# Output projection of the token mixers by pairs of column blocks, three of eight k-tile pairs with seven block products

## The chip, the cores and the metric

The kernel runs on one core of a Trainium2 chip. The metric is device microseconds from the first to the last instruction of that core, the median of several runs; the kernel before took 1666.72 us (three runs, 1664.29 to 1666.83). A profile is one execution, recorded by the hardware profiler; its times are microseconds from the start of its span. TensorE is PE in the rows (PEld its weight loads), VectorE is DVE, ScalarE is ACT, GpSimd is POOL, SyncE is SP.

## The reference, cut to what matters

One decoder layer on 256 tokens of width 2048, in float32. The change touches the lines marked with arrows.

```python
mixed = g_m * (y_m @ w_up_m) + g_r * (y_r @ w_up_r) + g_s * (y_s @ w_up_s)
h = x + mixed @ w_out                                    # <- output projection, 2048 x 2048
hn = rmsnorm(h, norm_ffn_g)
h = h + (silu(hn @ ffn_w_gate) * (hn @ ffn_w_up)) @ ffn_w_down   # <- gate and up: 2048 x 5632 each
h = h + (p @ ple_w_proj) * sigmoid(rmsnorm(h, norm_ple_g) @ ple_w_gate)
out = rmsnorm(h, final_norm_g)
```

## The kernel before

**Precision.** Every float32 operand is split into a high part, rounded to the matmul's type by a cast on ACT, and a low part, the difference, made on DVE. A product is three matmuls of 128x512: high x high, low x high, high x low. `split` (L190) does this for activations, `chunk` (L113) for weights; `mm2` (L139) issues the three matmuls in two parts, the third after the low part of the weights is due.

**Weights.** All weights lie in one array `wall` in the order in which they are used, cut into chunks of 1 MB: four tiles of 128x512. `load` (L102) brings one with a single DMA on SP's queue into a ring of three raw buffers. A chunk is split in two halves of 128x1024, each into a `whi` and a `wlo` buffer of which there are three each, so splitting can run some half chunks ahead of PE and no further. `layout` (L1392) writes the array on the host.

**The output projection (L1178 to L1186).** The mixed activations, transposed and split, are `mT[n]` (`mh`, `ml`). Four column blocks of 512 follow one another. For each, two tiles of x are loaded into `h` by ACT's queue, `gemm_tm` (L156) goes over 16 k-tiles in four chunks and two token tiles, 96 matmuls into two PSUM banks of the pool `mm` (four banks, so the next block has two others), DVE adds the banks onto `h`, and `h_block` (L1157) prepares the next stage: a sum of squares on ACT (`jk`), eight transposes on PE into two banks of the pool `sm` (four banks), and their splits, four `hhi` on ACT and four `hlo` on DVE, each 128x256. After the last block `rstd_of` (L1172) gives the norm's factors, with one operation on POOL.

**The FFN's gate and up (L1212 to L1307).** Eleven blocks, each one block of gate columns beside one of up columns. K is taken in eight pairs `u` of k-tiles, in the order `ORDER = (3, 4, 0, 5, 1, 6, 2, 7)`, one chunk for each. For `u` in `SEVEN = (0, 1, 2)` the 2x2 block product is formed with seven block products instead of eight (Winograd's form): `seven` (L1232) makes sums of the weight tiles, two on POOL (L1240, L1244; `tsum`) and two on DVE, and splits 7 tiles in place of 4; the activations' sums are made once before the first block (L1213 to L1222: `af`, four `sf`, then the split into `sh` and `sl`). Such a chunk takes 21 matmuls, a plain one 24. The plain products and three of the seven go to the four banks of `mm` (M2, M4, M3, M8), the others to the four banks of `sm` (M1, M7, M5, M6). After u=2 the latter are merged by one copy on ACT and four adds on DVE; after the last chunk four more adds on DVE bring in M2, M4, M3, M8. Then the gating (`sg`: two tanh on ACT, four operations on DVE), eight transposes and four copies into `hid`.

**The order of the work.** The Tile framework schedules at build time: each engine gets its instructions in an order chosen from their priority (program order; what stands under `high_priority`, such as loading and splitting weights and the merges, goes first) and from when its operands and buffers are ready. Buffers of one pool and tag are handed out and waited for by semaphores. The pool `b2` (L95, `t2`) holds 16 tiles of 128x512: `h`, `jk`, `af`, `sf`, `m1s`, `u`, `v`, `sg` and others. The pools `mp` and `pb` of the mixing part are closed at L1193 and L1194, and those of the FFN (`hid`, `dn`, `gu`) take their place.

Of the kernel before, what the change touches and what calls it, by code (L numbers as in the profile page):

```python
# [9 lines left out]
F32 = mybir.dt.float32  # L10
# [7 lines left out]
FFN = 5632  # L18
S5Q = 2
NKT = 16  # L20
# [17 lines left out]
ORDER = (3, 4, 0, 5, 1, 6, 2, 7)  # L38
SEVEN = (0, 1, 2)
# [35 lines left out]
def trunk(ctx: ExitStack, tc: tile.TileContext, xT, x, pT, wall, vecs, csts, s5b, s5c, gfin, out, dbg=None):  # L75
# [114 lines left out]
    def split(hi, lo, src, gain=None):  # L190
# [4 lines left out]
        else:  # L195
            nc.scalar.activation(out=hi, in_=src, func=AF.Identity if not isinstance(gain, float) else AF.Copy, scale=gain)
            nc.vector.scalar_tensor_tensor(out=lo, in0=src, scalar=gain, in1=hi.bitcast(F32), op0=ALU.mult, op1=ALU.subtract)

# [979 lines left out]
    for n in range(4):  # L1178
        xb = []
        for t in range(2):  # L1180
            h[t, n] = t2("h")
            nc.scalar.dma_start(out=h[t, n], in_=x[t * 128:(t + 1) * 128, n * 512:(n + 1) * 512])
        ps = gemm_tm(lambda k: mT[k // 4][0][:, k % 4, :], lambda k: mT[k // 4][1][:, k % 4, :], NKT)
        for t in range(2):
            tt(h[t, n], h[t, n], ps[t], ALU.add)
        h_block(n, hT, "gffn", ssq1)  # L1186
# [18 lines left out]

    SF = {}  # L1212
    for u in SEVEN:  # L1213
        af = t2("af").rearrange("p (a t) -> p a t", a=2)
        sf = t2("sf").rearrange("p (a t) -> p a t", a=4)
        tt(af, hh[:, 2 * u:2 * u + 2, :].bitcast(F32), hl[:, 2 * u:2 * u + 2, :].bitcast(F32), ALU.add)
        tt(sf[:, 0], af[:, 0, TS[1]], af[:, 1, TS[1]], ALU.add)
        tt(sf[:, 1], sf[:, 0], af[:, 0, TS[0]], ALU.subtract)
        tt(sf[:, 2], af[:, 0, TS[0]], af[:, 0, TS[1]], ALU.subtract)
        tt(sf[:, 3], af[:, 1, TS[0]], sf[:, 1], ALU.subtract)  # L1220
        SF[u] = tuple(gu.tile([128, 4, 128], F32R, name=q + "%d" % u) for q in ("sh", "sl"))
        split(*SF[u], sf)  # L1222

    def tiled(r):

        n = r.shape[1]
        hi = ring.tile([128, 2, 512], F32R, name="whi", tag="whi", bufs=3)[:, 0:n]
        lo = ring.tile([128, 2, 512], F32R, name="wlo", tag="wlo", bufs=3)[:, 0:n]
        split(hi, lo, r)
        return [(hi[:, q], lo[:, q]) for q in range(n)]  # L1230

    def seven():  # L1232

        if not loaded:
            load()
        raw, _ = loaded.pop(0)
# [11 lines left out]
    def A(u, t, k):  # L1248
        return hh[:, 2 * u + k, TS[t]], hl[:, 2 * u + k, TS[t]]

    for b in range(11):
# [3 lines left out]
        def prods(ops, last):  # L1255

            n_ = {q: max(i for i, o in enumerate(ops) if o[0] == q) for q in {o[0] for o in ops}}
            for part in range(2):
                for i, (q, a, w) in enumerate(ops):
                    mm2(M[q], *a, *w, part, q not in done, last and part == 1 and i == n_[q], True)  # L1260
                    if part == 0:
                        done.add(q)
# [242 lines left out]
```

## Time and profile before

| what | value |
|---|---|
| median of three runs | 1666.72 us (1664.29 to 1666.83) |
| the profiled execution | 1664.86 us |
| its span, first to last instruction | 1663.1 us |
| granted TensorE clock, mean | 0.998 of full speed |
| PE / PEld / DVE / ACT / POOL busy | 1641.0 / 1380.4 / 1276.8 / 908.7 / 184.8 us |
| output projection, its first matmul to the first of the FFN | 742.32 to 835.15 us |
| first FFN block | 835.15 to 878.97 us |

Busy time is the time in which an engine had an instruction at work. Ends of matmuls are modelled, so their spacing, the distance from one start to the next, says more than their duration. A number behind an arrow in a row is the time that an engine sat idle before the instruction, with what released it.

### The profile page before, as it was taken

How to read it: one execution, taken by the hardware profiler on the slowest of the kernel's cores; microseconds unless marked ns; L12 is line 12 of the kernel's file. 1: busy time of each engine (PE TensorE's matmuls, PEld its weight loads, DVE VectorE, ACT ScalarE, POOL GpSimd, SP SyncE). 2: the span in 40 equal slices, each digit the busy share in tenths (PEclk: the TensorE clock that was granted, in tenths of full speed). 3: DMA queues.
4: the chain of work that ended last, by engine and by line, in shares of the span. 5: the costliest groups of instructions: out<-in, count | busy, mean ns of one | idle time of the engine just before them, and what ended most of it. 6: DMA issues, size and time to landing. Idle time of an engine off the chain costs nothing.

```text
span 1663.1 us, 23487 instructions
## 1 busy us (share of the span) xinstructions
PE 1641.0 (99%) x9255; PEld 1380.4 (83%) x9255; DVE 1276.8 (77%) x1590; ACT 908.7 (55%) x1141; POOL 184.8 (11%) x131
## 2 busy tenths in 40 slices
PE   8999999999999999999999999999999999999997
PEld 8999889987888888888877888888888888888886
DVE  6999776969988545575589988888888867666565
ACT  6465566555645434444465555555555656656454
POOL 1100100100000000000032322332233000000000
PEclk9999999999999999999999999999999999999999
DMA  9655544555454444555544555555555655555553
GB/s 363 196 171 175 171 152 183 189 187 190 164 194 159 149 158 152 178 190 194 213 176 181 190 198 203 202 203 192 189 190 190 232 184 197 180 200 185 219 186 118
DMA packets 49455, 313.69 MB, mean 189 GB/s; under 512 B 5824, under 2 KB 9152, under 8 KB 12736
## 3 DMA queue, kind: packets, MB, share of 16 engines
q1 hardware_dynamic: 43488, 304.59, 50.7%
q0 software_dynamic: 3840, 3.15, 1.1%
q10 hardware_dynamic: 2016, 4.46, 0.8%
q8 instruction: 72, 1.18, 0.3%
q14 instruction: 39, 0.32, 0.1%
HBM read 306.93 MB, written 2.10 MB: 186 GB/s over the span
## 4 chain that ended last, share of the span: by engine, by line
PE 94%; DVE 3%; issue 1%; ACT 1%; DMA 1%; POOL 0%; SPq 0%; POOLq 0%; DVEq 0%
PE mm L142 23%; PE mm L143 23%; PE mm L145 23%; PE mm L149 4%; PE mm L152 4%; PE mm L150 4%; PE M L145 2%; PE M L142 2%; PE M L143 2%; DVE wlo L129 1%; DMA raw<-in_wall 1%; PE sm L544 1%; DVE wlo L194 1%; PE sm L1306 0%; PE mm L135 0%
## 5 line engine op out<-in xcount | busy, mean ns | idle before, releaser
L128 ACT CAST whi<-raw 128x1024 fp32r<-128x1024 f32 (+1 forms) x496 | 518.1, 1049 | 552.5 <-PE mm L143 393.4
L129 DVE TENSOR_TENSOR wlo<-raw,whi 128x1024 fp32r<-128x1024 f32 (+1 forms) x496 | 612.2, 1238 | 240.2 <-ACT whi L128 221.4
L143 PE MATMUL mm<-whi,alo 128*128 128x512 f32 x512 | 201.2, 393 | 0.0
L142 PE MATMUL mm<-whi,ahi 128*128 128x512 f32 x512 | 201.0, 393 | 0.0
L142 PE MATMUL mm<-whi,hhi 128*128 128x512 f32 x506 | 198.1, 392 | 0.3 <-DVE m1s L219 0.3
L143 PE MATMUL mm<-whi,hlo 128*128 128x512 f32 x506 | 196.8, 389 | 0.0
L149 PE MATMUL mm<-ahi,whi 128*128 128x256 f32 x576 | 143.3, 286 | 7.8 <-ACT whi L128 7.8
L145 PE MATMUL mm<-wlo,hhi 128*128 128x512 f32 x506 | 146.5, 393 | 0.8 <-DVE wlo L194 0.8
L150 PE MATMUL mm<-alo,whi 128*128 128x256 f32 x576 | 142.7, 285 | 0.0
L145 PE MATMUL mm<-wlo,ahi 128*128 128x512 f32 x512 | 139.2, 392 | 0.0
L142 PE MATMUL mm<-whi,dh 128*128 128x512 f32 x352 | 130.2, 389 | 0.0
L143 PE MATMUL mm<-whi,dl 128*128 128x512 f32 x352 | 130.2, 389 | 0.0
L149 PEld LDWEIGHTS mm<-ahi,whi 128*128 128x128 f32 x576 | 111.4, 194 | 8.8 <-ACT whi L128 8.0
L145 PEld LDWEIGHTS mm<-wlo,hhi 128*128 128x128 f32 x506 | 94.9, 188 | 24.0 <-DVE wlo L194 4.7
L142 PEld LDWEIGHTS mm<-whi,hhi 128*128 128x128 f32 x506 | 95.0, 188 | 23.1 <-issue 3.8
L142 PEld LDWEIGHTS mm<-whi,ahi 128*128 128x128 f32 x512 | 96.1, 188 | 21.2 <-issue 1.2
L143 PEld LDWEIGHTS mm<-whi,alo 128*128 128x128 f32 x512 | 96.1, 188 | 20.9 <-issue 1.2
L145 PEld LDWEIGHTS mm<-wlo,ahi 128*128 128x128 f32 x512 | 95.6, 188 | 20.6 <-issue 0.4
L150 PEld LDWEIGHTS mm<-alo,whi 128*128 128x128 f32 x576 | 111.4, 194 | 0.4 <-issue 0.4
L143 PEld LDWEIGHTS mm<-whi,hlo 128*128 128x128 f32 x506 | 95.0, 188 | 19.6
L1244 POOL TENSOR_TENSOR tsum<-raw,tsum 128x512 f32<-128x512 f32 x33 | 86.8, 2629 | 115.6 <-DVE tsum L219 110.4
L1240 POOL TENSOR_TENSOR tsum<-raw 128x512 f32<-128x512 f32 x33 | 56.0, 1696 | 381.9 <-PE mm L145 177.5
(536 smaller groups left out, 2842.0 us busy)
## 6 DMA issues: line engine op xcount, KB each, us to landing
raw<-in_wall SPq DMA_DIRECT2D x283, 1024.0 KB, 4.8
xrow<-in_x SPq DMA_DIRECT2D x2, 1024.0 KB, 8.7
h<-in_x ACTq DMA_DIRECT2D x8, 256.0 KB, 3.2
xraw<-in_xT SPq DMA_DIRECT2D x3, 512.0 KB, 10.7
ub<-Bh POOLq DMA_DIRECT2D x16, 64.0 KB, 3.8
ub<-uh POOLq DMA_DIRECT2D x16, 64.0 KB, 3.7
gft<-in_gfin ACTq DMA_DIRECT2D x1, 1024.0 KB, 6.0
out_dram<-fin SPq DMA_DIRECT2D x4, 256.0 KB, 3.2
```

The lines of the kernel that those rows point to most:

```text
L128: nc.scalar.copy(out=hi[:, q, :], in_=r)
L129: nc.vector.tensor_tensor(out=lo[:, q, :], in0=r, in1=hi[:, q, :].bitcast(F32), op=ALU.subtract)
L142: nc.tensor.matmul(ps, ah, wh, start=first, stop=False, skip_group_check=skip)
L143: nc.tensor.matmul(ps, al, wh, start=False, stop=False, skip_group_check=skip)
L145: nc.tensor.matmul(ps, ah, wl, start=False, stop=last, skip_group_check=skip)
L149: nc.tensor.matmul(ps, wh, ah, start=first, stop=False, skip_group_check=skip)
L150: nc.tensor.matmul(ps, wh, al, start=False, stop=False, skip_group_check=skip)
L152: nc.tensor.matmul(ps, wl, ah, start=False, stop=last, skip_group_check=skip)
L194: nc.vector.tensor_tensor(out=lo, in0=src, in1=hi.bitcast(F32), op=ALU.subtract)
L544: nc.tensor.matmul(psy[32 * j:32 * j + 32, a * 256:(a + 1) * 256], cc[:, ri, js_, :], G["s5x"][q][ri][:, a, :], start=ri == 0, stop=ri == ...
L1240: nc.gpsimd.tensor_tensor(out=ts_[:, 0], in0=raw[:, 3], in1=raw[:, 0], op=ALU.subtract)
L1244: nc.gpsimd.tensor_tensor(out=ts_[:, 2], in0=raw[:, 1], in1=ts_[:, 1], op=ALU.subtract)
```

## The change

The output projection takes two column blocks at a time, as the FFN takes gate and up: one function `gemm_pair` now serves both. Three of eight k-tile pairs go by seven products. The sums of the mixed activations (`MS`) are made ahead of the first pair; their split parts lie in tiles of the mixing part that are no longer read (`room_pb`). The results are added onto `h` in two steps: the merged M1, M7, M5, M6 after u=2, and M2, M4, M3, M8 at the end. `h_block` runs for both blocks of a pair after the pair. The sums of h for the FFN (`SF`) stand where they stood. The FFN's first block takes its k pairs in the order `ORDER0`, the other ten in `ORDER`; `tsum` of the FFN moves from the pool `gu` to the pool `hid`. On the host the chunks of `w_out` and of the first FFN block are laid out accordingly.

```diff
 ORDER = (3, 4, 0, 5, 1, 6, 2, 7)
+ORDER0 = (3, 0, 1, 2, 4, 5, 6, 7)
 SEVEN = (0, 1, 2)
...
+    def sums(sf, a):
+        tt(sf[:, 0], a[:, 0, TS[1]], a[:, 1, TS[1]], ALU.add)
+        tt(sf[:, 1], sf[:, 0], a[:, 0, TS[0]], ALU.subtract)
+        tt(sf[:, 2], a[:, 0, TS[0]], a[:, 0, TS[1]], ALU.subtract)
+        tt(sf[:, 3], a[:, 1, TS[0]], sf[:, 1], ALU.subtract)
+    def sums_of(hi, lo, room):
+        af = t2("af").rearrange("p (a t) -> p a t", a=2)
+        sf = t2("sf").rearrange("p (a t) -> p a t", a=4)
+        tt(af, hi.bitcast(F32), lo.bitcast(F32), ALU.add)
+        sums(sf, af)
+        split(*room, sf)
+        return room
...
+    def gemm_pair(A, S, order, by7, room, prep=None, onto=None):
...
+                if end:
+                    with tc.high_priority():
+                        m1, u2, u3, u4, v4 = (t2(q) for q in ("m1s", "u2", "u3", "u4", "v4"))
+                        nc.scalar.copy(out=m1, in_=M[1])
+                        tt(u2, M[6], m1, ALU.add)
+                        tt(u3, M[7], u2, ALU.add)
+                        tt(u4, M[5], u2, ALU.add)
+                        tt(v4, M[5], u3, ALU.add)
+                    res = (m1, u3, u4, v4)
+                    if onto is not None:
+                        for o, r in zip(onto, res):
+                            tt(o, o, r, ALU.add)
+                        res = onto
...
+        with tc.high_priority():
+            for o, q in zip(res, (2, 4, 3, 8)):
+                tt(o, M[q], o, ALU.add)
+        return res
...
-    for n in range(4):
-        xb = []
-        for t in range(2):
-            h[t, n] = t2("h")
-            nc.scalar.dma_start(out=h[t, n], in_=x[t * 128:(t + 1) * 128, n * 512:(n + 1) * 512])
-        ps = gemm_tm(lambda k: mT[k // 4][0][:, k % 4, :], lambda k: mT[k // 4][1][:, k % 4, :], NKT)
-        for t in range(2):
-            tt(h[t, n], h[t, n], ps[t], ALU.add)
-        h_block(n, hT, "gffn", ssq1)
+    MS = {u: sums_of(*(q[:, 2 * (u % 2):2 * (u % 2) + 2, :] for q in mT[u // 2]), room_pb(u)) for u in SEVEN}
+    for n in (0, 2):
+        for m in (n, n + 1):
+            for t in range(2):
+                h[t, m] = t2("h")
+                nc.scalar.dma_start(out=h[t, m], in_=x[t * 128:(t + 1) * 128, m * 512:(m + 1) * 512])
+        gemm_pair(lambda u, t, k: tuple(q[:, 2 * (u % 2) + k, TS[t]] for q in mT[u // 2]), sum_of(MS), ORDER, SEVEN, tsum_t8,
+                  onto=(h[0, n], h[1, n], h[0, n + 1], h[1, n + 1]))
+        for m in (n, n + 1):
+            h_block(m, hT, "gffn", ssq1)
...
-    SF = {}
-    for u in SEVEN:
...
+    SF = {u: sums_of(hh[:, 2 * u:2 * u + 2, :], hl[:, 2 * u:2 * u + 2, :], room_of(gu, "sf%d" % u)) for u in SEVEN}
     for b in range(11):
...
+        c11, c21, c12, c22 = gemm_pair(act_of(hh, hl), sum_of(SF), ORDER if b else ORDER0, SEVEN, tsum_of(hid_p))
...
-    blocks(a["w_out"][0])
+    wo = a["w_out"][0]
+    for n in (0, 1024):
+        pair(wo[:, n:n + 512], wo[:, n + 512:n + 1024], ORDER)
```

The parts of `gemm_pair` that are left out are the FFN block's loop as it was (L1252 to L1292), and `tiled` and `seven` have only moved; `seven` now takes its `tsum` tile from the function `room`.

## Rows read from the trace of the kernel before

**Rows 1.** From the page: busy time, share of the span and instruction count of PE and DVE; the granted clock in 40 slices of the span, in tenths; the chain that ended last, by engine.
```profile
PE 1641.0 (99%) x9255; PEld 1380.4 (83%) x9255; DVE 1276.8 (77%) x1590; ACT 908.7 (55%) x1141; POOL 184.8 (11%) x131
PEclk9999999999999999999999999999999999999999
PE 94%; DVE 3%; issue 1%; ACT 1%; DMA 1%; POOL 0%; SPq 0%; POOLq 0%; DVEq 0%
```
**Rows 2.** Busy time by stretches: the output projection, the first 26 us of the FFN, its first and second block, and a settled stretch of one block's length. Columns: stretch and its length, busy us and instructions of PE, PEld, DVE, ACT and POOL, granted clock, DMA share, GB/s.
```profile
742.32:835.15 92.83, 92.83 (x425) 76.25 (x424) 52.31 (x59) 44.78 (x61) 0.00 (x0) 1.00 0.56 199
835.15:861.46 26.31, 25.72 (x116) 20.56 (x115) 26.19 (x43) 16.59 (x24) 11.70 (x6) 1.00 0.44 158
835.15:878.97 43.82, 43.22 (x192) 34.74 (x191) 41.62 (x60) 27.09 (x36) 15.12 (x7) 1.00 0.50 180
878.97:922.00 43.03, 42.30 (x187) 34.16 (x188) 40.41 (x41) 24.66 (x30) 10.72 (x6) 1.00 0.52 188
1008.00:1051.00 43.00, 43.00 (x193) 35.03 (x193) 37.71 (x41) 24.41 (x29) 12.96 (x6) 1.00 0.53 198
```
**Rows 3.** Waits of PE over the whole span, those on DVE: us in total, times, longest.
```profile
PE mm L145 <- DVE wlo L194: 1.3, 4, 0.5
PE M L142 <- DVE hlo L197: 0.4, 1, 0.4
PE mm L142 <- DVE m1s L219: 0.3, 2, 0.2
```
**Rows 4.** PE in order of time in the output projection: start, us, engine, line, operation, operands, count. Eight transposes between matmuls.
```profile
743.46 1.04 PE L365 MATMUL sm<-ct,gate 128*128 128x128 f32 x8
744.25 0.47 PE L143 MATMUL mm<-whi,ml 128*128 128x512 f32 x1
744.56 0.39 PE L142 MATMUL mm<-whi,mh 128*128 128x512 f32 x1
```
**Rows 5.** DVE's costliest groups in the settled stretch 1008 to 1051: line, operands, shape, count, busy us, mean ns, idle before.
```profile
L129 DVE TENSOR_TENSOR wlo<-raw,whi 128x1024 fp32r<-128x1024 f32 x11 | 14.4, 1318 | 0.0
L194 DVE TENSOR_TENSOR wlo<-raw,whi 128x1024 fp32r<-128x1024 f32 x6 | 8.2, 1400 | 0.0
L194 DVE TENSOR_TENSOR wlo<-tsum,whi 128x1024 fp32r<-128x1024 f32 x3 | 4.0, 1343 | 2.3 <-PE mm L145 2.3
L219 DVE TENSOR_TENSOR raw<-raw 128x512 f32<-128x512 f32 x3 | 2.1, 690 | 2.4 <-POOL tsum L1240 2.4
L219 DVE TENSOR_TENSOR tsum<-raw 128x512 f32<-128x512 f32 x3 | 2.1, 690 | 0.0
L194 DVE TENSOR_TENSOR wlo<-tsum,whi 128x512 fp32r<-128x512 f32 x3 | 2.1, 688 | 0.1
```
**Rows 6.** DVE in order of time at two settled block ends: the add that frees M2's bank at 1052.02, and the merges up to the same add one block later.
```profile
1052.02 0.68 DVE L219 TENSOR_TENSOR m1s<-mm,m1s 128x512 f32<-128x512 f32 x1
...
1090.21 0.69 DVE L219 TENSOR_TENSOR u<-M,m1s 128x512 f32<-128x512 f32 x1 [0.44 <-PE M L145]
1090.82 1.22 DVE L129 TENSOR_TENSOR wlo<-raw,whi 128x1024 fp32r<-128x1024 f32 x1
1091.95 1.28 DVE L219 TENSOR_TENSOR u<-M,u 128x512 f32<-128x512 f32 x2
...
1094.88 0.68 DVE L219 TENSOR_TENSOR m1s<-mm,m1s 128x512 f32<-128x512 f32 x1
```
**Rows 7.** PE in order of time at the second of these block ends: the last four matmuls of one block and the first of the next.
```profile
1094.70 1.07 PE L145 MATMUL mm<-wlo,hhi 128*128 128x512 f32 x4
1095.71 0.47 PE L142 MATMUL mm<-whi,hhi 128*128 128x512 f32 x1
```
**Rows 8.** DVE in order of time in the first FFN block.
```profile
837.75 0.68 DVE L219 TENSOR_TENSOR af<-hhi,hlo 128x512 f32<-128x512 f32 x1
...
842.04 0.48 DVE L219 TENSOR_TENSOR sf<-af 128x128 f32<-128x128 f32 x2
842.44 0.68 DVE L219 TENSOR_TENSOR af<-hhi,hlo 128x512 f32<-128x512 f32 x1
843.04 0.87 DVE L197 SCALAR_TENSOR_TENSOR hlo<-sm,vt,hhi 128x256 fp32r<-128x256 f32 x2
843.83 0.60 DVE L219 TENSOR_TENSOR sf<-af,sf 128x128 f32<-128x128 f32 x1
...
856.88 3.45 DVE L194 TENSOR_TENSOR wlo<-raw,whi 128x1024 fp32r<-128x1024 f32 x2
```
**Rows 9.** ACT and its DMA queue (ACTq) in order of time, at three places: the end of the first column block, the last `jk` of the output projection, and the end of the eleventh FFN block.
```profile
766.89 0.63 ACT L1161 ACTIVATE jk<-h 128x512 f32<-128x512 f32 x1 [0.35 <-DVE h L219]
...
767.50 0.34 ACTq L1182 DMA_DIRECT2D h<-in_x  x1
...
836.48 0.62 ACT L1161 ACTIVATE jk<-h 128x512 f32<-128x512 f32 x1
...
1311.75 0.72 ACT L225 ACTIVATE sg<-u,hrs 128x512 f32<-128x512 f32 x1 [0.76 <-DVE u L219]
1311.75 0.34 ACTq L1310 DMA_DIRECT2D praw<-in_pT  x1
```
**Rows 10.** POOL's groups from 835 to 1310 us: count, busy us, mean ns, idle before.
```profile
L1244 POOL TENSOR_TENSOR tsum<-raw,tsum 128x512 f32<-128x512 f32 x33 | 86.8, 2629 | 115.6 <-DVE tsum L219 110.4 <-DVE rs1m L216 5.2
L1240 POOL TENSOR_TENSOR tsum<-raw 128x512 f32<-128x512 f32 x33 | 56.0, 1696 | 381.9 <-PE mm L145 177.5 <-DMA raw<-in_wall 161.2 <-DVE wlo L194 43.3
```

More of the change, by code (lines that the diff above doesn't have):

```diff
@@ new lines, in tiled, with seven @@
+    def tiled(r):
+        n = r.shape[1]
+        hi = ring.tile([128, 2, 512], F32R, name="whi", tag="whi", bufs=3)[:, 0:n]
+        lo = ring.tile([128, 2, 512], F32R, name="wlo", tag="wlo", bufs=3)[:, 0:n]
+        split(hi, lo, r)
+        return [(hi[:, q], lo[:, q]) for q in range(n)]
+    def seven(room):
+        if not loaded:
+            load()
+        raw, _ = loaded.pop(0)
+        with tc.high_priority():
+            ts_ = room()
+            out_ = [tiled(raw[:, 0:2])]
+            nc.gpsimd.tensor_tensor(out=ts_[:, 0], in0=raw[:, 3], in1=raw[:, 0], op=ALU.subtract)
+            tt(raw[:, 3], raw[:, 2], raw[:, 3], ALU.subtract)
+            out_.append(tiled(raw[:, 2:4]))
+            tt(ts_[:, 1], raw[:, 3], raw[:, 0], ALU.add)
+            nc.gpsimd.tensor_tensor(out=ts_[:, 2], in0=raw[:, 1], in1=ts_[:, 1], op=ALU.subtract)
+            out_ += [tiled(ts_[:, 0:2]), tiled(ts_[:, 2:3])]
+        return out_
@@ L1203, in trunk @@
     hh, hl = hT
-    SF = {}
-    for u in SEVEN:
[L1214 to L1236, printed above, removed]
-        with tc.high_priority():
-            ts_ = gu.tile([128, 3, 512], F32, name="tsum", tag="tsum", bufs=2)
-            out_ = [tiled(raw[:, 0:2])]
-            nc.gpsimd.tensor_tensor(out=ts_[:, 0], in0=raw[:, 3], in1=raw[:, 0], op=ALU.subtract)
-            tt(raw[:, 3], raw[:, 2], raw[:, 3], ALU.subtract)
-            out_.append(tiled(raw[:, 2:4]))
-            tt(ts_[:, 1], raw[:, 3], raw[:, 0], ALU.add)
-            nc.gpsimd.tensor_tensor(out=ts_[:, 2], in0=raw[:, 1], in1=ts_[:, 1], op=ALU.subtract)
-            out_ += [tiled(ts_[:, 0:2]), tiled(ts_[:, 2:3])]
-        return out_
@@ L1435, in blocks, with pair @@
             block(w[:, n * 512:(n + 1) * 512])
+    def pair(l, r, order):
+        l, r = (q.reshape(-1, 2, 128, 512) for q in (l, r))
+        for u in order:
+            chunks.append(np.stack([l[u, 0], l[u, 1], r[u, 1], r[u, 0]], axis=1).reshape(128, 2048))
     block(w_in[:, 6088:6600])
@@ L1453, in layout @@
     blocks(a["w_up_r"][0])
[L1454 to L1455 removed]
+    wo = a["w_out"][0]
+    for n in (0, 1024):
+        pair(wo[:, n:n + 512], wo[:, n + 512:n + 1024], ORDER)
     for n in range(11):
         c = slice(n * 512, (n + 1) * 512)
[L1458 to L1459 removed]
+        pair(a["ffn_w_gate"][0][:, c], a["ffn_w_up"][0][:, c], ORDER if n else ORDER0)
     blocks(a["ffn_w_down"][0])
```

91 lines of the change are left out of this document (45 added, 46 removed).

## The prediction

> **What bounds the kernel now.** I read the page's busy times first, then the table by stretches, the waits of TensorE, and last the order of single instructions around the end of the output projection. TensorE (PE) is busy 99% of the span and holds 94% of the chain that ended last; VectorE (DVE) is busy 77% [rows 1]. So a matmul removed is worth its spacing, unless PE must wait for something that it does not wait for today. The mean hides where such a wait could come from: in the output projection DVE works 52.31 of 92.83 us, in a settled FFN block 37.71 of 43.00, and in the first 26.31 us of the FFN 26.19, so there it has nothing left [rows 2]. PE idles 0.59 us in that last stretch and not at all in the settled block [rows 2]; its named waits on DVE are few and short [rows 3]. The clock is granted at 1.00 throughout. The change therefore takes time from PE in a stage where PE is the limit, and brings DVE work into the stage and into the very stretch where DVE is full.
>
> **Removed on PE.** Before, the stage has 16 k-tiles x 2 token tiles x 3 x 4 column blocks = 384 matmuls. After, each pair has 5 x 24 + 3 x 21 = 183, together 366: 18 fewer. Spacing: eight transposes take 743.46 to 744.25 plus 0.08 of the next step, 0.11 each; the stage's 92.83 us less 40 of them (4.4) over 384 is 0.230 us [rows 2, 4]. 18 x 0.230 = **4.15 us saved**. In the settled FFN block the same sum gives (43.00 - 0.9) / 185 = 0.228 [rows 2]; should the new pairs run at that, 366 x 0.0027 = 1.0 more is saved. I take 0, since the stationary tiles (mh, ml) stay; the ends are 0 and 1.0. Weight loads go with their matmuls and ran beside them. The weight DMAs (16 of 1 MB), the h loads and the 32 transposes of h stay in number, so they cost nothing as long as their cover, three raw buffers ahead, holds.
>
> **Prices on DVE.** Queued back to back, an op starts 0.60 us after the one before it (128x512), 1.13 (128x1024), 0.40 (hlo) or 0.20 (128x128) [rows 6, 8]. So one seven-product chunk costs 3 x 1.13 + 3 x 0.60 = 5.2 us on DVE against 21 x 0.23 = 4.8 on PE; a plain chunk costs 2.3 against 5.5. The FFN works because ORDER puts them in turn. A settled block has 10 x 1.13 + 3 x 5.2 + 12 x 0.60 = 34.1 us by these prices, yet shows 37.71 [rows 2, 5]: while GpSimd (POOL) works, DVE's ops stretch (two splits in 3.45 instead of 2.3 [rows 8]), 3.6 / 3 = 1.2 us per seven-chunk.
>
> So a seven-chunk takes 6.4 us of DVE, by the row. Were DVE and POOL never to work at once, it would take 5.2 + 1.70 + 2.63 (POOL's two ops, as they lasted [rows 10]) = 9.5. The settled block speaks against that: 13 us of POOL stretch its DVE by 3.6, not by 13 [rows 2]. The Trainium skill, "SBUF — State Buffer", section "Who interferes with whom", states the stricter case: a VectorE instruction with two SBUF inputs and a GpSimd instruction that reads SBUF shut each other out for a whole instruction. By that rule the sum below would grow by 3 x 3.1 us; the trace agrees with it only in part.
>
> **Sums of the mixed activations, before the first pair.** Per u: 0.60 + 4 x 0.20 + 0.60 = 2.0 us of DVE and one cast on ScalarE; 6.0 in all, beside the last gate and mh/ml work. Nearest row: the FFN's first block has this list, the same ORDER, and lasted 43.82 us [rows 2], against 42.86 for a settled one (1052.02 to 1094.88, from the add of M2 to the next block's [rows 6]). I take that, **+1.0**; ends 0 and 3.
>
> **The end of a pair.** At a settled FFN boundary the merge chain starts at 1090.21, the add that frees M2's bank ends at 1095.56, and the next block's first matmul starts at 1095.71, 0.1 later than its predecessors allow [rows 6, 7]. No slack. The change puts four adds (onto h, 4 x 0.60 = 2.4 us) ahead of that add; behind it on DVE wait the splits of the next two half chunks. Some splits that now stand between the merges can slide. Ends 0 and 2.4 each; I take 1.1 at both pair ends, **+2.2**.
>
> **The FFN's first block in ORDER0.** This is the largest term. After u=3 come three seven-chunks in a row, and they need the sums of h (SF). Those cannot move far forward: tiles of the pool b2 are handed out in program order. Seen in the rows: the buffers for h's second block are free once the mixed tiles have been read, early in the stage, yet its load is issued at 767.50, right after the first block's jk (766.89); af starts at 837.75 right after the last jk (836.48); the load of praw, which depends on nothing, waits for the last sg at 1311.75 [rows 8, 9]. After the change the last jk still stands behind the second pair's end (call it T0). From T0 until the last product of u=2, DVE has: two last adds onto h 1.2; second half of u=3 1.13; three seven-chunks 3 x 6.4 = 19.2; eight hlo, now of two blocks, 3.2; SF 6.0; the rs chain 1.3. Sum 32.0 us. PE has 24 + 63 - 3 = 84 matmuls x 0.228 + 16 transposes x 0.11 = 21.0. The difference is 11.0. I take off 1.1 for the half chunk that DVE may be ahead, and 0.9 for hlo that only u=6 and 7 need: **+9.0**. The transposes add a wait of their own: their four PSUM tiles are the same four buffers as M1, M7, M5, M6, so u=0 cannot start before the first is split. Lower end 1 (SF done under the second pair, late hlo last: 32.0 - 6.0 - 1.6 - 1.1 - 1.3 = 22 against 21); upper end 18 (DVE and POOL never at once, 3.1 more for each of three chunks). I take 9, since the nearest row, today's first 26 us, shows DVE full from the boundary on with a list that PE's 26 us just covers [rows 2], and the new list is 11 us longer than its cover.
>
> **Gone.** Today's first FFN block loses 43.82 - 42.86, so **-1.0**; that block is costed anew above.
>
> **Sum.** -4.15 + 1.0 + 2.2 + 9.0 - 1.0 = +7.05 us. The profiled execution took 1664.86 us (span 1663.1); the runs' median is 1666.72, 1.86 above. That gives 1671.9 against the one and 1673.8 against the other; I say **1673.0, slower**. What a measurement can tell from no change is 0.2%, 3.3 us: faster is below 1663.4, slower above 1670.1.
>
> **Rivals.** (a) *Hidden sums, no change.* The second pair has 37.7 - 2.4 (sg) + 2.4 (onto) + 3.2 (hlo) = 40.9 us of DVE in 43.9 of PE. If SF finds room there, the first block stalls 2.4 instead of 9: -4.15 + 1.0 + 2.2 + 2.4 - 1.0 = +0.45, 1667.2. Against it stands the order of the b2 tiles; for it, that PE's and DVE's order is made by a scheduler that may place things better than a list shows. Chance 0.22. (b) *Faster.* DVE's lead (up to two half chunks) takes up the boundaries and most of the run of three, as today's first block overran its cover and cost PE only 0.59 us [rows 2]: new stalls of 2.0 in all, less today's 1.0, against 4.15 and the 1.0 of the closer spacing: -4.15, 1662.6. It decides as soon as all new stalls of PE together stay under 1.8 us (1.0 + 4.15 - 3.3). Chance 0.18. (c) *DVE and POOL never at once.* The run of three then costs 9.0 + 3 x 3.1 = 18.3 instead of 9.0: 1682. The settled block bears that out only in part (3.6 of 13 us). The page named above states it as the rule. Chance 0.05. That leaves 0.55 for the forecast, whose own range is 1670 to 1680.
>
> **How the numbers follow.** Faster 0.18 is (b), the same 0.22 is (a), slower 0.60 is the forecast and (c). The range goes from 1664, which leaves out some two thirds of (b), to 1680, which leaves out (c) and a little of the forecast's end: about 0.18 outside.
>
> **What would show it.** Right: 366 matmuls in the projection; its two pairs about 43 to 46 us each; af still behind the last jk; a first FFN block near 52 us, with PE's idle time released by DVE (sl, wlo, hlo) around u=0 to 2; later blocks at 43.0. Wrong: a first block under 45 us, or af, sf and sl in the middle of the second pair (then (a)); no idle PE at all (then (b)); or pairs far over 46 us, by which the sums before the first pair or the onto adds were sized too small.

## The result and the profile after

The changed kernel takes 1683.49 us (median of four runs, 1682.84 to 1685.07) against 1666.61 us of the kernel before, timed beside it: a ratio of 1.0106, 95% interval 1.0090 to 1.0122. That is 16.9 us slower; the forecast was 1673.0, its range ended at 1680. The profiled execution took 1685.07 us, its span is 1683.1, 20.0 longer than that of before.

The busy times from the page of the changed kernel, against [rows 1]. PE runs 18 matmuls fewer, as it should, and is busy 5.7 us longer; DVE works 40.4 us more.
```profile
PE 1646.7 (98%) x9237; PEld 1381.7 (82%) x9237; DVE 1317.2 (78%) x1648; ACT 920.1 (55%) x1158; POOL 208.2 (12%) x143
```
The table by stretches of the changed kernel, against [rows 2] (columns as there): ten microseconds far ahead of the changed part; the projection; the first 26.3 us of the FFN; its first block up to the add that frees M2's bank; and a settled block.
```profile
160.00:170.00 10.00, 10.00 (x38) 7.67 (x38) 8.85 (x16) 3.51 (x5) 0.00 (x0) 0.86 0.59 211
744.53:840.30 95.77, 89.54 (x401) 71.67 (x400) 83.70 (x104) 53.25 (x70) 25.28 (x11) 1.00 0.56 196
840.30:866.60 26.30, 17.21 (x61) 12.27 (x60) 26.30 (x46) 12.10 (x24) 8.54 (x7) 0.81 0.23 85
840.30:896.06 55.76, 46.65 (x188) 36.10 (x187) 48.74 (x68) 28.32 (x42) 12.13 (x7) 0.91 0.41 150
1008.00:1051.00 43.00, 43.00 (x193) 34.99 (x193) 37.73 (x41) 24.42 (x29) 13.05 (x6) 1.00 0.55 196
```
Three things are to be seen. DVE's work in the projection rose from 52.31 us to 83.70, and PE, which had no idle time there, has 6.2 us. In the first 26.3 us of the FFN, DVE has not one free moment, PE works only 17.21 us, and its clock is granted at 0.81. The settled block is as before, so the eleven blocks share one form and only the first are hurt. The projection starts 2.2 us later than before (744.53 against 742.32): at 160 to 170 us the clock was granted at 0.86. That dip is not the change's: the kernel late_plain below, with nearly the same changed projection, starts it at 741.88, and before_early, which has no pairs, has the dip too (0.83 at 160 to 170 us).

DVE's adds that free M2's bank, in the first four FFN blocks of the changed kernel, in order of time.
```profile
896.06 0.69 DVE L343 TENSOR_TENSOR m1s<-mm,m1s 128x512 f32<-128x512 f32 x1 [1.09 <-PE mm L146]
941.42 0.68 DVE L343 TENSOR_TENSOR m1s<-mm,m1s 128x512 f32<-128x512 f32 x1
985.72 0.68 DVE L343 TENSOR_TENSOR m1s<-mm,m1s 128x512 f32<-128x512 f32 x1
1028.85 0.68 DVE L343 TENSOR_TENSOR m1s<-mm,m1s 128x512 f32<-128x512 f32 x1
```
In the kernel before the same adds stood at these times.
```profile
878.15 0.68 DVE L219 TENSOR_TENSOR m1s<-mm,m1s 128x512 f32<-128x512 f32 x1
922.53 0.68 DVE L219 TENSOR_TENSOR m1s<-mm,m1s 128x512 f32<-128x512 f32 x1
965.90 0.68 DVE L219 TENSOR_TENSOR m1s<-mm,m1s 128x512 f32<-128x512 f32 x1
1009.14 0.68 DVE L219 TENSOR_TENSOR m1s<-mm,m1s 128x512 f32<-128x512 f32 x1
```
From the projection's first matmul to the last of them it took 266.82 us before and 284.32 after: **17.5 us** of the 20.0, made of 2.94 in the projection (95.77 against 92.83), 12.76 in the first block (55.76 against 43.00), and 1.8 in the next three. I use this stretch, "start to fourth block", to compare all kernels, because it leaves out the chance dip ahead of it.

PE's named waits over the changed kernel's span, against [rows 3].
```profile
PE mm L146 <- DVE wlo L195: 8.9, 7, 3.3
...
PE mm L146 <- DVE wlo L130: 2.3, 1, 2.3
PE mm L143 <- ACT whi L194: 2.0, 2, 1.5
...
PE M L143 <- DVE hlo L198: 1.2, 1, 1.2
```
PE waits for the low parts of weights, above all those of the seven-product chunks (L195), that is, for DVE. What DVE did meanwhile, in order of time from the end of the second pair (answers to [rows 8]; the last matmul of the projection is over at 840.3):
```profile
840.57 2.32 DVE L130 TENSOR_TENSOR wlo<-raw,whi 128x1024 fp32r<-128x1024 f32 x1
842.80 1.75 DVE L343 TENSOR_TENSOR h<-h,u 128x512 f32<-128x512 f32 x1
844.47 1.21 DVE L195 TENSOR_TENSOR wlo<-raw,whi 128x1024 fp32r<-128x1024 f32 x1
845.61 0.68 DVE L343 TENSOR_TENSOR h<-h,v 128x512 f32<-128x512 f32 x1
846.21 0.68 DVE L343 TENSOR_TENSOR h<-mm,h 128x512 f32<-128x512 f32 x1
...
848.01 1.27 DVE L343 TENSOR_TENSOR h<-mm,h 128x512 f32<-128x512 f32 x2
...
852.13 1.59 DVE L343 TENSOR_TENSOR af<-hhi,hlo 128x512 f32<-128x512 f32 x1
...
868.96 2.92 DVE L195 TENSOR_TENSOR wlo<-tsum,whi 128x1024 fp32r<-128x1024 f32 x2
...
874.07 1.81 DVE L195 TENSOR_TENSOR wlo<-tsum,whi 128x1024 fp32r<-128x1024 f32 x2
```
Five adds onto h of the projection (842.80 to 849.2) stand inside the FFN's first block; `af` of the FFN follows only at 852.13, and DVE is through with the three seven-chunks at 875.9, 35.6 us after the pair's end.

### The profile page after: what moved, and what is told of

The parts are those of the page before. It is cut to its first block, busy times and chain, and to the rows that moved or that the text cites. A ratio compares the mean times of both kernels' runs of the same rounds, so it can differ in the third digit from the quotient of the medians.

```text
span 1683.1 us, 23561 instructions
## 1 busy us (share of the span) xinstructions
PE 1646.7 (98%) x9237; PEld 1381.7 (82%) x9237; DVE 1317.2 (78%) x1648; ACT 920.1 (55%) x1158; POOL 208.2 (12%) x143
## 4 chain that ended last, share of the span: by engine, by line
PE 91%; DVE 4%; issue 1%; DMA 1%; ACT 1%; POOL 1%; SPq 0%; POOLq 0%; ACTq 0%; DVEq 0%
PE mm L143 22%; PE mm L144 22%; PE mm L146 22%; PE mm L150 4%; PE mm L153 4%; PE mm L151 4%; PE M L143 2%; PE M L146 2%; PE M L144 2%; DMA raw<-in_wall 1%; DVE wlo L130 1%; POOL tsum L259 1%; PE sm L668 1%; DVE wlo L195 1%; DVE h L343 1%
## 5 line engine op out<-in xcount | busy, mean ns | idle before, releaser
L129 ACT CAST whi<-raw 128x1024 fp32r<-128x1024 f32 (+1 forms) x484 | 505.6, 1049 | 529.7 <-PE mm L144 369.7
L130 DVE TENSOR_TENSOR wlo<-raw,whi 128x1024 fp32r<-128x1024 f32 (+1 forms) x484 | 601.2, 1247 | 218.7 <-ACT whi L129 196.4
L259 POOL TENSOR_TENSOR tsum<-raw,tsum 128x512 f32<-128x512 f32 x39 | 99.9, 2561 | 137.4 <-DVE tsum L343 137.4
L194 ACT CAST whi<-raw 128x1024 fp32r<-128x1024 f32 x78 | 82.1, 1052 | 56.1 <-PE mm L144 39.7
## 6 DMA issues: line engine op xcount, KB each, us to landing
xraw<-in_xT SPq DMA_DIRECT2D x3, 512.0 KB, 10.3
```

What stands on the lines that cost most here:

```text
L129: nc.scalar.copy(out=hi[:, q, :], in_=r)
L130: nc.vector.tensor_tensor(out=lo[:, q, :], in0=r, in1=hi[:, q, :].bitcast(F32), op=ALU.subtract)
L194: nc.scalar.copy(out=hi, in_=src)
L259: nc.gpsimd.tensor_tensor(out=ts_[:, 2], in0=raw[:, 1], in1=ts_[:, 1], op=ALU.subtract)
```

## The experiments

The table gives for each kernel the ratio to the kernel before, timed beside it on the same chip (with its 95% interval), and from its profile the projection's length, the first FFN block's up to the add that frees M2, the start to the fourth block and its difference to the kernel before, all read as above. A profile is a single execution: changed, order_plain, no_sf and filler differ only behind the projection, and their projections range from 93.31 to 96.67 us. So differences of less than some 3 us between two profiles are not told apart; where they matter, the ratios are given beside them.

| kernel | ratio | projection | first block | start to fourth block | against before |
|---|---|---|---|---|---|
| before | 1 | 92.83 | 43.00 | 266.82 | 0 |
| changed | 1.0106 (1.0090 to 1.0122) | 95.77 | 55.76 | 284.32 | +17.5 |
| order_plain | 1.0052 (1.0032 to 1.0072) | 94.18 | 48.44 | 273.59 | +6.8 |
| order0_alone | 1.0072 (1.0057 to 1.0087) | 92.84 | 50.02 | 277.08 | +10.3 |
| onto_late | 1.0073 (1.0058 to 1.0088) | 91.53 | 53.47 | 278.35 | +11.5 |
| no_sf | 1.0064 (1.0049 to 1.0079) | 93.31 | 48.93 | 274.14 | +7.3 |
| no_ms | 1.0089 (1.0074 to 1.0103) | 94.91 | 55.10 | 282.74 | +15.9 |
| filler | 1.0103 (1.0089 to 1.0117) | 96.67 | 54.75 | 285.10 | +18.3 |
| late_plain | 1.0045 (1.0031 to 1.0059) | 89.72 | 53.77 | 273.04 | +6.2 |
| sums_early | 1.0041 (1.0027 to 1.0056) | 99.11 | 46.16 | 275.03 | +8.2 |
| pairs_only | 1.0018 (1.0009 to 1.0027) | 92.06 | 47.64 | 269.67 | +2.9 |
| no_sums | 0.9999 (0.9990 to 1.0008) | 89.32 | 45.23 | 265.47 | -1.4 |
| vector_sums | 1.0045 (1.0031 to 1.0058) | 91.16 | 52.58 | 273.93 | +7.1 |
| before_early | 0.9984 (0.9975 to 0.9993) | 92.84 | 41.70 | 264.04 | -2.8 |

Two theories stood against each other at first: the loss sits in the first FFN block, because ORDER0 takes three chunks in a row that DVE cannot feed (A), or in the projection, with sums and merges that the forecast priced too low (B).

**order_plain** and **order0_alone** take the order of the first block away from the changed kernel, and put it alone into the kernel before.

```diff
-ORDER0 = (3, 0, 1, 2, 4, 5, 6, 7)
+ORDER0 = ORDER
```


> The changed kernel with the first FFN block back in ORDER (weights laid out to match); everything else as changed. Theory A (VectorE's list in the first block is too long for the three seven-chunks in a row): the first block falls from 58 us to 47 to 50, TensorE's clock stays at 1.00, total 1673 to 1676. Theory B (what is late is the second pair's h_block, and any order waits for it): u=4 now waits for hlo of the second pair, the block stays at 56 or more, total 1681 to 1685.

> The kernel before with nothing but its first FFN block in ORDER0. Theory A: VectorE must do three seven-chunks, the sums of h and four hlo (30 us) against some 20 us of TensorE; the block grows from 43.8 to 51 to 54, total 1674 to 1677. Theory B (only the two h_blocks of a pair make it late): the block stays under 46, total 1666 to 1669.

The first fell by 10.7 us (start to fourth block), the second rose by 10.3: the order of the first block costs about the same with and without the rest of the change. Of order0_alone, the first 26.3 us of the FFN and the first block:
```profile
834.95:861.25 26.30, 20.66 (x76) 15.28 (x75) 25.52 (x43) 13.57 (x22) 15.82 (x7) 0.81 0.28 102
834.95:884.97 50.02, 44.38 (x180) 34.93 (x179) 42.08 (x60) 25.30 (x34) 15.82 (x7) 0.90 0.45 163
```
The picture of the changed kernel is there with nothing changed but the order: DVE all but full, PE idle for a fifth of the time, the clock at 0.81. DVE's work in the projection and the first block together is 94.4 us, 1.3 more than before, so here it is its place that costs, and not its amount. PE's longest wait comes by a detour, though, for a cast on ACT of a sum that POOL needed 4.06 us for, beside a DVE without a gap (the three rows, from the wait back):
```profile
847.03 0.80 PE L143 MATMUL mm<-whi,hhi 128*128 128x512 f32 x1 [4.17 <-ACT whi L194]
846.36 0.62 ACT L194 CAST whi<-tsum 128x512 fp32r<-128x512 f32 x1 [3.01 <-POOL tsum L1245]
842.27 4.06 POOL L1245 TENSOR_TENSOR tsum<-raw,tsum 128x512 f32<-128x512 f32 x1 [3.51 <-DVE rs1m L217]
```
And order_plain stays 6.8 us slower than the kernel before, so the rest of the change loses too, and theory A alone is not enough.

**onto_late** moves the four adds onto h behind the adds that free the banks.

```diff
                     res = (m1, u3, u4, v4)
-                    if onto is not None:
-                        for o, r in zip(onto, res):
-                            tt(o, o, r, ALU.add)
-                        res = onto
...
                 tt(o, M[q], o, ALU.add)
+        if onto is not None:
+            for o, r in zip(onto, res):
+                tt(o, o, r, ALU.add)
+            res = onto
```


> The changed kernel, with the four adds onto h moved behind the four adds that free M2, M4, M3, M8 (the same number of adds, off the way of the banks). Theory A: both pair ends give back 1 to 2.4 us each, total 1679 to 1682. Theory B (the ends are late because VectorE is behind altogether): the splits stay as late, total 1682.5 to 1684.5.

The projection lost 4.2 us (91.53 against 95.77), about twice the 2.2 of the forecast's term, and the whole stretch 6.0 (by the ratios 5.5), a little more than theory A's 1 to 2.4 at each of two ends. The four profiles with early adds have 93.31 to 96.67 us in the projection, onto_late and late_plain, with late ones, 91.53 and 89.72.

**no_sf** and **no_ms** leave the sums of h, and those of the mixed activations, out.

```diff
-    SF = {u: sums_of(hh[:, 2 * u:2 * u + 2, :], hl[:, 2 * u:2 * u + 2, :], room_of(gu, "sf%d" % u)) for u in SEVEN}
+    SF = {u: tuple(q[:, 2 * u:2 * u + 2, :].rearrange("p a (b t) -> p (a b) t", b=2) for q in (hh, hl)) for u in SEVEN}
```


> The changed kernel without the sums of h for the FFN: the tiles of h's own splits stand in their place, so 6 us of VectorE and 2 us of ScalarE are left out before the first block (the FFN's numbers are then others). Theory A: the first block falls by 5 to 7 us, total 1676 to 1679. Theory B (GpSimd's sums of the weights, shut out by VectorE, are what TensorE waits for): it falls by under 2 us, total 1681.5 to 1684.

> The changed kernel with the sums of the mixed activations left out: the split tiles of the mixed activations themselves stand in for them as operands, so the number of matmuls is the same and only the DVE, ACT work of the sums ahead of the first pair is gone (the output is not the reference's). Theory A (the sums on DVE hold up the first pair: they crowd the weights' low parts and starve POOL's weight sum, which took 9.02 us beside them in place of about 2.2): the 9.02 us operation falls to 2 to 3 us, the stalls of PE at 761 to 764 us go, the projection (95.77 us) becomes 2 to 3.5 us shorter, the time about 1681. Theory B (the forecast's price): about 1 us shorter, 1682.5. Theory C (the projection lost its time in the ends of the pairs alone): no difference.

Without SF the stretch is 10.2 us shorter, but that profile is of an execution 4.5 us below the median of its runs; by the ratios it is 7.0, for some 6 us of DVE's work. Without MS it is only 1.6, though PE's waits in the projection fell from 6.2 to 3.8 us (94.91 less 91.08 busy). A lower granted clock there (0.98) took part of that back, so these two figures put the price of MS at 1.6 to 2.4; by the ratios it is 2.8, with intervals of 2.5 us to either side on each, so it is not clear of nothing. The waiting of POOL that theory A of no_ms names is plain in the changed kernel. POOL's second weight sum there, in order of time:
```profile
751.64 9.02 POOL L259 TENSOR_TENSOR tsum<-raw,tsum 128x512 f32<-128x512 f32 x1 [7.59 <-DVE tsum L343]
...
766.75 2.21 POOL L259 TENSOR_TENSOR tsum<-raw,tsum 128x512 f32<-128x512 f32 x1 [4.86 <-DVE tsum L343]
```
The first of the two lasts four times as long as the second; in no_ms the same one is short:
```profile
748.60 1.68 POOL L259 TENSOR_TENSOR tsum<-raw,tsum 128x512 f32<-128x512 f32 x1 [3.74 <-DVE tsum L343]
```

**filler** asks what the clock costs. PE stood idle 3.35 us before a matmul at 845.74 and 2.95 us before one at 860.64, and after each ran matmuls at a spacing of 0.43 us instead of 0.228. Added matmuls fill both waits. The changed kernel's three waits of over 1 us in the first block:
```profile
845.74 0.50 PE L146 MATMUL mm<-wlo,hhi 128*128 128x512 f32 x1 [3.35 <-DVE wlo L195]
855.47 0.47 PE L143 MATMUL M<-whi,hhi 128*128 128x512 f32 x1 [1.22 <-DVE hlo L198]
860.64 0.80 PE L146 MATMUL mm<-wlo,hhi 128*128 128x512 f32 x1 [2.95 <-DVE wlo L195]
```

```diff
                     if part == 0:
                         done.add(q)
+                        for _ in range(extra):
+                            nc.tensor.matmul(M[q], a[0], w[0], start=False, stop=False, skip_group_check=True)
...
-                prods([(2, A(u, 0, 1), b21)], last)
+                prods([(2, A(u, 0, 1), b21)], last, more.get((u, 2), 0))
...
-                prods([(4, A(u, 1, 1), t4_)], last)
+                prods([(4, A(u, 1, 1), t4_)], last, more.get((u, 4), 0))
...
+        ... more={} if b else {(0, 2): 14, (0, 4): 13})
```


> The changed kernel with 27 added matmuls in the first FFN block, which do no useful work (they add a product again into a bank, so the output is not the reference's): 14 ahead of the matmul that waits 3.35 us for a low part at 845.7 us, 13 ahead of the one that waits 2.95 us at 860.6 us, each 0.228 us, so about as long as the two waits. They keep PE busy where it stood idle, and delay nothing else than PE. Theory A (a part of the block's loss is the clock, granted 0.81 in its first 26 us, which falls because PE stood idle; about 20 matmuls then go at 0.43 us in place of 0.228): the granted clock of the stretch rises to over 0.9, the block gets 2 to 4 us shorter in spite of the added matmuls, the time about 1680 to 1682. Theory B (the block waits for DVE, and the slow matmuls only fill time in which it would wait anyway): the block's length stays within 1 us or grows, the time 1683 to 1686, whatever the clock does.

Its first 26.3 us and its first block:
```profile
840.37:866.67 26.30, 20.30 (x91) 14.69 (x90) 26.30 (x47) 11.92 (x25) 10.08 (x7) 1.00 0.23 85
840.37:895.12 54.75, 48.75 (x215) 38.01 (x214) 48.39 (x68) 27.97 (x42) 15.21 (x7) 1.00 0.44 153
```
The clock is back at 1.00 and the block is 1.0 us shorter, the time the same. So about 20 matmuls at half clock, some 4 us of PE, cost about 1 us at most: PE would have waited for DVE in that time. One matmul shows it. At full clock PE comes to it earlier, waits 2.62 us for the same low part in place of 1.22, and starts it 15.2 us after the block's first matmul, as before:
```profile
855.55 0.47 PE L143 MATMUL M<-whi,hhi 128*128 128x512 f32 x1 [2.62 <-DVE hlo L198]
```
Theory B of this run holds, and in this block the clock is an effect of the loss, not its cause.

**late_plain** undoes both the order and the early adds; **sums_early** also makes the sums of h between the two pairs.

> The changed kernel with two things undone: the first FFN block in the order of the ten others, and the four adds onto h of each pair moved behind the adds that free the banks. Apart the two gave -9.4 us and -5.6 us against the changed kernel. Theory A (the two are separate charges, one in the first FFN block, one in the projection's two pair ends): they add up, the projection near 90 us and the first FFN block near 48 us, the time 1668 to 1670. Theory B (both only empty the same backlog of DVE, which either undoes): the time is that of the better of the two or up to 2 us below it, 1672 to 1674.

```diff
         for m in (n, n + 1):
             h_block(m, hT, "gffn", ssq1)
+        if n == 0:
+            sf_ = {}
+            for u in SEVEN:
+                af, sf_[u] = t2("af").rearrange("p (a t) -> p a t", a=2), t2("sf").rearrange("p (a t) -> p a t", a=4)
+                tt(af, *(q[:, 2 * u:2 * u + 2, :].bitcast(F32) for q in hT), ALU.add)
+                sums(sf_[u], af)
```


> As the kernel with the two things undone, and also the sums of h for the FFN (af and the four sf for each of three u, without their splits) made on DVE between the two pairs of the projection, where the trace of the changed kernel has DVE idle for about 12 of 96 us, in place of in the first FFN block. Theory A (DVE's list is what makes the first FFN block long; what is taken off it there and put where DVE has idle time is gained): the first FFN block 3 to 5 us shorter than with the two things undone alone, the time 1664 to 1666, at or below the kernel before. Theory B (the second pair is as full of DVE work as the block): what the block gains the projection loses, the time within 1 us of the kernel with the two things undone.

Of late_plain, the projection and the first block:
```profile
741.88:831.60 89.72, 89.07 (x400) 71.58 (x398) 84.36 (x103) 52.95 (x70) 27.89 (x11) 1.00 0.58 210
831.60:885.37 53.77, 47.70 (x197) 37.26 (x198) 47.15 (x70) 29.44 (x42) 11.75 (x7) 0.94 0.42 150
```
Of sums_early, the same two stretches:
```profile
744.16:843.27 99.11, 91.62 (x399) 72.52 (x398) 87.98 (x121) 54.67 (x73) 34.81 (x12) 0.98 0.53 191
843.27:889.43 46.16, 43.49 (x196) 35.43 (x197) 42.67 (x52) 26.43 (x38) 11.89 (x7) 1.00 0.49 171
```
These two told most. In late_plain the projection has all of the matmuls' gain (89.72, with 0.65 us of idle PE), and over the whole stretch it lands 0.6 us from order_plain, which is no difference: what the projection gave up came back in the first block, which is 53.77 against 48.44. In sums_early the block shrinks by 7.6 us and the projection grows by 9.4. (A clock granted at 0.98 in the projection, about 2 us of 99.11, is part of the 9.4.) By the ratios, 1.0045 and 1.0041, the two are the same. Theory B of both runs holds: the same backlog, moved to and fro. PE's longest waits in the projection of sums_early (4.0 us in three) are for casts on ACT, and the last of them comes from DVE by way of POOL, which is held off once more:
```profile
811.48 9.35 POOL L259 TENSOR_TENSOR tsum<-raw,tsum 128x512 f32<-128x512 f32 x1 [4.61 <-DVE tsum L343]
820.86 0.62 ACT L194 CAST whi<-tsum 128x512 fp32r<-128x512 f32 x1 [5.25 <-POOL tsum L259]
```

**pairs_only** keeps the pairs and undoes the seven products of the projection, with their sums (and the order); **no_sums** is late_plain without either set of sums; **vector_sums** is late_plain with POOL's weight sums given to DVE; **before_early** is the kernel before with its sums of h made after the second column block. The diff is that of pairs_only.

```diff
-    MS = {u: sums_of(*(q[:, 2 * (u % 2):2 * (u % 2) + 2, :] for q in mT[u // 2]), room_pb(u)) for u in SEVEN}
...
-        gemm_pair(..., sum_of(MS), ORDER, SEVEN, tsum_t8,
+        gemm_pair(..., None, ORDER, (), tsum_t8,
```


> The changed kernel with the pairs of column blocks kept and the seven block products of the projection undone: eight plain k-tile pairs (384 matmuls again), no sums of the mixed activations, the four banks added onto h at the pair's end; the first FFN block in the order of the ten others. Theory A (the DVE work of the seven products is the charge; DVE's busy time in the projection rose from 52 to 84 us): DVE near 52 us in the projection, PE without waits, the projection 92.8 to 93.5 us, the FFN's first block 44 to 46 us because two blocks' transposes and low parts stand at the boundary in place of one, the time 1667 to 1669, less than the changed kernel and less than the kernel with all matmuls saved and two things undone (1673.1). Theory B (the pairing itself is the charge: h_block of both blocks late, at the pair's end): the projection 95 us or more or the first block over 48, the time over 1671.

> The kernel with the two things undone (order of the first FFN block, adds onto h late), and both sets of sums of activations (of the mixed ones and of h) left out: the split tiles themselves stand in as operands, so the number of matmuls is the same and about 12 us of DVE's work is gone (the output is not the reference's). Theory A (DVE's list is the bound from the projection's start to the end of the first FFN block, and nothing else is wrong with the change): the first block falls from 53.8 to 44 to 47 us, the projection stays near 89.5, and the saved matmuls show at last: 1662 to 1666. Theory B (the waits come from the form itself, its chains of sum, cast and low part between POOL, ACT and DVE, whatever DVE's load): the first block stays above 49 us and the time above 1668.

> The kernel with the two things undone, and the two weight sums of each seven-product chunk that POOL makes given to DVE, in the projection and in the first FFN block. Theory A (POOL's sums cost by contention: they stretch DVE's work by about 1.2 us a chunk, which is what two more adds of 0.60 us cost DVE, and POOL itself is held off for up to 9 us while DVE is full, and PE waits for those sums): DVE's busy time stays within 4 us, the waits of PE get shorter, the time 1668 to 1671. Theory B (DVE's list is the bound and every operation added to it lengthens it): 9 chunks x 1.2 us = 11 us more of DVE, the first block 2 to 5 us longer, the time 1674 to 1679.

> The kernel before, with one thing moved: the sums of h for the FFN (af and four sf for each of three u, without their splits) made after the second of the projection's four column blocks in place of after the fourth, where DVE is busy 52 of 93 us. Theory A (the 26.2 of 26.3 us for which DVE is full at the FFN's start cost PE something, seen as 0.6 us of idle time there and as block steps of 43.0, 44.4 and 43.4 us where settled blocks take 42.9): the three steps fall to 43, the time 1664 to 1665.5, 1 to 2 us below the kernel before, at the edge of what can be told. Theory B (those steps come from something else): no difference.

Of pairs_only, the projection and the first block:
```profile
743.55:835.61 92.06, 92.06 (x420) 75.52 (x418) 50.89 (x55) 43.12 (x57) 0.00 (x0) 1.00 0.55 194
835.61:883.25 47.64, 44.63 (x197) 36.32 (x196) 41.80 (x64) 27.14 (x38) 16.82 (x7) 0.96 0.46 165
```
With the seven products gone PE has no idle time in the projection. The pairing itself costs 2.9 us (by the ratio 1.5 to 4.5), at the first block: the time, 1668.95, is theory A's, the block is longer than its 44 to 46. PE's idle time there, 3.0 us where it had 0.59, is two waits on DVE, for a low part of h and for that of a sum of h:
```profile
851.71 0.47 PE L143 MATMUL M<-whi,sf0h 128*128 128x512 f32 x1 [0.83 <-DVE hlo L198]
854.35 0.50 PE L144 MATMUL mm<-whi,sf0l 128*128 128x512 f32 x1 [2.18 <-DVE sf0l L195]
```
So it is the `hlo` of two blocks and SF that PE waits for there. That is read from these rows; no run takes one of them away.

Of no_sums:
```profile
743.15:832.47 89.32, 88.81 (x400) 71.60 (x398) 79.06 (x89) 51.91 (x67) 20.10 (x12) 1.00 0.56 198
832.47:877.70 45.23, 43.64 (x197) 35.48 (x198) 40.60 (x50) 27.53 (x39) 12.15 (x7) 1.00 0.48 173
```
Taking some 12 us of DVE's work away gives 7.6 us of time (by the ratios 7.7): by its profile 1.4 us below the kernel before, by the median of its runs (1665.57 against 1665.89) the same. It is 4.2 us below pairs_only, but pairs_only still makes SF, which is worth 2.8 by before_early; so the 18 matmuls bring between 1.4 and 4.2 where DVE can nearly keep up; these runs don't narrow that, and 1.4 alone would not be clear of noise.

Of vector_sums, the projection, and its costliest DVE group:
```profile
744.30:835.46 91.16, 89.79 (x399) 71.42 (x398) 84.69 (x115) 53.21 (x70) 0.00 (x0) 1.00 0.59 206
```
```profile
L130 DVE TENSOR_TENSOR wlo<-raw,whi 128x1024 fp32r<-128x1024 f32 x21 | 25.5, 1217 | 1.4 <-PE M L146 1.4
```
The same group of late_plain's projection:
```profile
L130 DVE TENSOR_TENSOR wlo<-raw,whi 128x1024 fp32r<-128x1024 f32 x21 | 27.6, 1324 | 1.1 <-PE M L146 0.9 <-issue 0.2
```
Both theories were half right. DVE's work is 84.69 us against 84.36 and the time 1673.63 against 1673.12 (both 1.0045 of the kernel before): twelve more adds on DVE in the projection cost what the stretch by POOL had cost, and neither place is the better.

before_early is the only version that is clearly below both kernels: 1663.80 us against 1665.89, and its first three blocks take 41.70, 43.07 and 43.21 us. Its first stretches:
```profile
836.63:862.93 26.30, 26.30 (x121) 21.81 (x120) 23.56 (x30) 16.65 (x25) 7.93 (x6) 1.00 0.53 198
836.63:878.33 41.70, 41.70 (x189) 34.56 (x188) 37.96 (x44) 25.43 (x34) 10.14 (x7) 1.00 0.51 188
```
PE has no idle time at all there, where it had 0.59 us [rows 2].

## Why the prediction was right in direction and wrong in size

That it came out slower was not luck: the forecast's largest term, the run of three in the first block, is there without the rest of the change (order0_alone, 10.3 us). What failed is the size of the sum. Of some 10.5 us that it lacked (17.5 against 7.05), 3.9 lie in the projection (+2.94, where -4.15 + 1.0 + 2.2 stood) and 6.6 in the first four blocks (12.76 + 1.8, where 9.0 - 1.0 stood). Three terms failed: the end of a pair, the pairing, which was priced at nothing, and the list of the first block.

**Matmuls removed: right.** 18 fewer are counted, and where PE does not wait (late_plain, no_sums) the projection is 3.1 to 3.5 us shorter with its remaining idle time in it; 92.83 - 4.15 = 88.68, and PE's busy time there is 89.07 and 88.81.

**The sums before the first pair, +1.0: perhaps too low, within its ends.** no_ms gives 1.6 to 2.4, not clear of noise. The nearest row, the FFN's first block, was read too low: there moving the sums away gains 2.8 us (before_early; 2.1 by the medians), not the 1.0 that I read from one block's length. The two blocks after it, which took 44.38 and 43.37 us in the kernel before, carried the rest, and I had not counted them in.

**The end of a pair, +2.2: failed, by its place.** onto_late measures 4.2 in the projection. The second pair's first matmul starts at 791.44, so the pairs took 46.9 and 48.9 us, above the 43 to 46 that I had put, the sign that I had given for terms sized too small:
```profile
791.44 0.47 PE L143 MATMUL mm<-whi,mh 128*128 128x512 f32 x1
```
The row showed no slack at such an end, and I priced four adds against the one bank that they delay. They delay all that stands behind them on DVE: at the second pair's end two of these adds and three of the last ones came after the projection's last matmul (842.80 to 849.2).

**The pairing, priced at nothing beyond that: failed.** pairs_only shows 2.9 us with no more DVE work in the projection (50.89 us against 52.31): PE waits for `hlo` and for the sums of h at the first block.

**The first block in ORDER0, +9.0 - 1.0: mechanism right, size off.** `af` comes at 852.13, behind the last `jk` (849.51), as [rows 8, 9] had suggested, and PE waits for wlo and hlo around u=0 to 2. I had forecast 52 us to the next block's first matmul; by the traces it is 898.81 - 840.30 = 58.5. The list of 32.0 us took 35.6. It held two adds onto h where five came, 1.8 us. It held 3.6 us for the stretch beside POOL, and six DVE instructions are each about 1.0 us longer than elsewhere, 6.0 in all (three are shown above: the split at 840.57, the add at 842.80 and `af` at 852.13). Against that, the rs chain took 0.3 where 1.3 stood. The 2.0 us taken off, for a half chunk of lead and for hlo not needed at once, were not there: DVE splits the second half of u=3 at 840.57, when PE has begun on that chunk, and all eight `hlo` are done before the last sums. With the two, 9.0 becomes 14.6 and the block 57.6; 0.9 us are left over. "Later blocks at 43.0" failed too: the second and third took 45.36 and 44.30, each 1 us over before.

**What joined these failures.** I summed separate charges, each against PE's time at its own place. The runs show DVE's work coming too late, by its amount and by its place. The amount: between the projection's start and the end of the first block it is 37 to 39 us more (132.4 us in the changed kernel, 130.1 in order_plain, 93.1 before), and with 12 us of it left out the loss of late_plain is gone (no_sums). The place: in order0_alone 10.3 us are lost with 1.3 us more of it. The amount alone nearly fits, for PE needs 131.7 us there after the change (135.83 - 4.15). But DVE idles 12.1 us in the changed projection (95.77 - 83.70) while PE waits there for 6.2. DVE's named waits in that stretch are for PE to have read a `wlo` buffer (4.3 us), for POOL's first weight sum (4.3) and for work on ACT (3.4). vector_sums takes the second away without gain; the others no run takes away.

The prices also hang on each other. In the path pairs_only (+2.9), late_plain (+6.2), order_plain (+6.8), changed (+17.5), the early adds cost 0.6 us under ORDER and 6.0 under ORDER0, the order 10.7 with early adds and 278.35 - 273.04 = 5.3 with late ones. By the ratios it is 1.2 and 5.5, 9.0 and 4.7, each ratio with an interval of 2 to 3 us to either side, so this is likely and not shown beyond doubt.

**The rivals.** (a) and (b) needed a DVE with room and fell. (c), DVE and POOL never at once, gave 1682, nearer to the measured time than the forecast, by luck: it prices the run of three at 18.3, which by itself costs 10.3 (order0_alone), a settled block of the changed kernel shows DVE 37.73 and POOL 13.05 us of 43.00, more than its length together, and with POOL's sums taken away from both stretches the time does not move (vector_sums). A rival's number that comes out is no evidence for its mechanism. **The clock**, which I took as 1.00 throughout, was granted at 0.81 in the first 26.3 us of the FFN; by filler it costs about 1 us at most.

Open: what of the pairing's 2.9 us is due to `hlo` and what to SF; what each of DVE's waits in the projection costs PE; why PE's granted clock dips now and then far from any edit.

## What to carry to other kernels

Before work is given to an engine that is "77% busy", add up its list over the whole run of neighbouring stages in which it cannot catch up, and then again up to each point at which the bounding engine needs a result: here 4 us taken from PE were paid with 37 to 39 us of DVE in the projection and the first FFN block, and the order of one block cost 10.3 us with hardly any more work. Where steps share one backlog their prices need not add, so test them in pairs as well as alone. The cheapest repair moves prepared work out of the full stretch into an emptier stage, and pays only as long as that stage stays emptier (2.1 us gained in before_early, nothing in sums_early).

## What the runs showed of the hardware

POOL and DVE hold each other off. One POOL add of 128x512 lasted 9.02 us while DVE went through more than ten instructions with two SBUF inputs each, without a gap from 751.5 to 759.5 us; it lasted 1.68 with the sums on DVE left out, and 9.35 again where sums_early filled DVE at 811 us. It is not always POOL that waits. In the changed kernel's first FFN block DVE has no gap from 840.3 to 875.9 either, and there a POOL add took 1.29 us and DVE's instruction beside it 1.59 (`af` at 852.13 above) where it takes 0.68 [rows 8]:
```profile
851.89 1.29 POOL L259 TENSOR_TENSOR tsum<-raw,tsum 128x512 f32<-128x512 f32 x1 [0.63 <-DVE tsum L343]
```
What decides between the two, these runs don't show. The Trainium skill, "SBUF — State Buffer", section "Who interferes with whom", says that such a DVE instruction and a GpSimd instruction that reads SBUF contend for a port that one of them holds for a whole instruction. Both kinds of rows agree with that; that a POOL add can be held off over many DVE instructions in a row is what they add.

PE's clock fell in the stretch in which PE had idled 3.35 and 2.95 us. The changed kernel was granted 0.83 at 840 to 850 us, 1.00 at 850 to 860 and 0.66 at 860 to 870; behind each of the two waits matmuls stand 0.43 us apart in place of 0.228, at the lower of the two levels, 1.2 GHz in place of 2.4. With the two waits filled by matmuls it stayed at 1.00. A granted clock below 1.00 in a stage with idle PE time can thus be a sign of the waits alone, and its price has to be tested before it is charged.
